# Weight sums of the first and the last chunk in a seven-product SwiGLU: other queue, other tiles, other order

## The chip, the core and the metric

The kernel runs on one core of a Trainium2 chip. The core has a matrix engine (TensorE, PE in the profile), a vector engine (VectorE, DVE), a scalar engine (ScalarE, ACT), GpSimd (POOL) and SyncE (SP), each with a queue of its own that it works through in order, and 16 DMA engines. [...] The metric is the device time of one execution in microseconds; the profile gives times within one execution, from the start of its span.

## The reference

The reference is an encoder trunk of two layers on one sequence of 512 tokens with 1024 features, in float32. Layer 0 mixes tokens with dilated window attention, layer 1 with a gated linear attention (GLA) in both directions. Behind each mixer stands a SwiGLU feed-forward network (FFN) with 2816 hidden features:

```python
for i in range(DEPTH):
    hn = rms_norm(h, attn_norm[i])
    h = h + mixer_i(hn)
    h = h + swiglu(rms_norm(h, ffn_norm[i]), ffn_w_gate_up[i], ffn_w_down[i])

def swiglu(h, w_gate_up, w_down):
    g, u = jnp.split(h @ w_gate_up, 2, axis=-1)
    return (jax.nn.silu(g) * u) @ w_down
```

## The kernel before

**Precision.** Each float32 operand is split into a high part (an ACT copy with rounding) and a low part (a DVE subtraction): `split`, L90 and L91. A product is three matmuls: high by high (L297), low weight by high (L298) and high weight by low (L299). Split weights live in three buffers each, `wh` and `wl`, so the split of a weight tile can run at most three tiles ahead of PE.

**Seven products.** `gate_up` computes `h @ [gate, up]` in six chunks of hidden features: chunks 0 to 4 of 512, chunk 5 (the last) of 256. A chunk is treated as a 2 by 2 block product, the tokens and the features of `h` being halved, and done with seven instead of eight block products of the Strassen kind. On the side of `h` the operands are A11, A12, A22 (pieces of `xs`) and four sums S1 to S4. On the side of the weights, DRAM holds four blocks for each chunk, and the sums of them are formed on the chip. In the order of the loop the products are:

| product | operand of h | weight, by `forms` | how the weight comes |
|---|---|---|---|
| 1 | A11 | `first` | chunk 0 and last: block 0 into `wf`; others: `wA` |
| 2 | A12 | `second` | block 1 into `wf` |
| 3 | S1 | `fifth` | `wA` = block 0 + block 2 |
| 4 | S2 | `sixth` | `wA` += `wC` (block 3), on DVE, L265 |
| 5 | S4 | `third` | `wC` (block 3); `wA` += block 1 is issued |
| 6 | S3 | `seventh` | `wB` = block 3 + block 2 |
| 7 | A22 | `fourth` | `wA` |

A product is 24 matmuls; weight tiles come in pairs of 128x1024. Loads are plain DMAs issued by SP (L225). Sums with a block from DRAM are DMAs that accumulate into the tile, issued by POOL (L230). An add waits until its tile's earlier load has landed and its earlier readers are done; all DMAs of POOL stand in one queue.

**The sums S1 to S4.** They are built once for each layer (`block_sums`), for four feature tiles of `h`: one ACT copy, four DVE operations of 256 columns and one split of 1024 columns for each tile, `sh` and `sl`. S1 to S4 of a tile are then ready together.

**Norm.** RMS norm is applied as a factor for each token behind the products. `add_square` sums squares of `h` into `acc` (ACT and DVE), `token_norm` sums over partitions on PE (L202) and takes the inverse root with small DVE and ACT steps (L108, L109 on ACT). The silu of each chunk (L356, L378), the product with the up half (L368, L380) and the four sums of partial results (L355, L367, L373) follow on ACT and DVE. `turn` transposes the finished half chunk on PE (L323) while the next chunk's products run.

**What sets the order.** The program is written once in the order above; a scheduler then orders each engine's queue by priority. `high_priority(offset=n)` moves what is issued inside it forward by n steps of the program; every `forms` step runs with AHEAD = 100, the first step of chunk 0 with 200 more. `issue_after(x)` keeps what is issued inside it behind instruction x. Tiles of a tag rotate through a fixed number of buffers, and a new phase (attention, FFN, GLA) lays its pools over those of the phase before; a tile that lies over an older one waits for that one's last reader. After the seven products `h` is stored to DRAM (`h_dram`, L352, by POOL), as its tiles are used for activations, and read back in `down`.

The lines that the prediction names: L90, L91 split; L97 load of other weights; L108, L109, L202, L205 norm; L150 sum of squares; L191 to L194 block sums; L225 load; L230 accumulating load; L265 sum of two weight tiles; L297 to L299 matmuls; L323 transposes; L337 copies of partial results; L352 store of `h`; L355, L356, L367, L368 sums, silu and product. L702 to L720 are attention, L784 is the residual sum behind the output projection.

Of the kernel before, what the change touches and what calls it, by code (L numbers as in the profile page):

```python
# [34 lines left out]
AHEAD = 100  # L35


class Trunk:
    def __init__(self, ctx, tc, ins):
        self.tc = tc  # L40
        self.nc = tc.nc
        self.ins = ins
        self.base = ctx.enter_context(tc.tile_pool(name="base", bufs=1))
# [9 lines left out]
    FFN = {"a": NH - KT, "sh": 4, "sl": 4, "wA": 4, "wB": 2, "g": 7, "Rc": 8}  # L53
# [4 lines left out]
    @contextmanager  # L58
    def phase(self, name, bufs):
        self.bufs = bufs  # L60
        with self.tc.tile_pool(name=name, bufs=1, reuse_waits="tile") as self.local:
            yield

    def t(self, tag, shape=(P, S), dt=F32):
        self.n += 1
        pool, bufs = (self.base, self.BASE) if tag in self.BASE else (self.local, self.bufs)
        return pool.tile(list(shape), dt, tag=tag, name=f"{tag}_{self.n}", bufs=bufs[tag])
# [18 lines left out]
    def split(self, src, shape, tag_h, tag_l):  # L86
        nc = self.nc
        hi = self.t(tag_h, shape, F32R)
        lo = self.t(tag_l, shape, F32R)
        nc.scalar.activation(hi, src, AF.Copy)  # L90
        nc.vector.tensor_sub(lo, src, hi.bitcast(F32))  # L91
        return hi, lo
# [89 lines left out]
    def block_sums(self, m):  # L182
        nc = self.nc
        stt = nc.vector.scalar_tensor_tensor
        c1 = self.cols[:, self.col0 + m:self.col0 + m + 1]
        c2 = self.cols[:, self.col0 + m + 4:self.col0 + m + 5]
        h2 = self.h[m + 4]
        t = self.t("g", (P, S))
        nc.scalar.activation(t, self.h[m], AF.Copy, scale=c1)
        f = self.t("g", (P, 4, 256))  # L190
        stt(f[:, 1], h2[:, 256:S], c2, t[:, 256:S], op0=ALU.mult, op1=ALU.subtract)  # L191
        nc.vector.tensor_sub(f[:, 0], t[:, 0:256], t[:, 256:S])
        stt(f[:, 2], f[:, 1], -1.0, t[:, 0:256], op0=ALU.mult, op1=ALU.subtract)
        stt(f[:, 3], h2[:, 0:256], self.minus[:, m:m + 1], f[:, 2], op0=ALU.mult, op1=ALU.subtract)  # L194
        hi, lo = self.split(f.rearrange("p a b -> p (a b)"), (P, 1024), "sh", "sl")
        return [(hi[:, i * 256:(i + 1) * 256], lo[:, i * 256:(i + 1) * 256]) for i in range(4)]

    def token_norm(self):
        nc = self.nc
        ss = self.p("t")  # L200
        for i in range(NT):
            nc.tensor.matmul(ss[:, i:i + 1], lhsT=self.acc[:, i * P:(i + 1) * P], rhs=self.ones[:, 0:1].bitcast(F32),  # L202
                             start=True, stop=True)
        v, r, tmp = (self.t("Rc", (P, 8)) for _ in range(3))
# [11 lines left out]
    def forms(self, dram, own, ahead=0):  # L216
        nc = self.nc
        n = dram.shape[1]
        raw = {}

        def load(block, tag, at=None):
            raw[tag] = []
            for i in range(n):
                w = self.t(at or tag, (P, 1024))
                nc.sync.dma_start(w, dram[block, i])  # L225
                raw[tag].append(w)

        def add(tag, block):
            for i in range(n):
                nc.gpsimd.dma_start(raw[tag][i], dram[block, i], accum_op=ALU.add)  # L230
# [19 lines left out]
        def second():  # L250
            if own:
                sums()
# [48 lines left out]
    def gate_up(self, layer, acts):  # L301
# [4 lines left out]
        weights.append(self.forms(self.ins["gate_up_last"][layer], True))  # L306
        first = next(weights[0])
        self.minus = self.t("Rc", (P, 8))
        DVE.tensor_scalar(self.minus[:, 0:4], self.cols[:, self.col0 + 4:self.col0 + 8], -1.0, None, op0=ALU.mult)
        sums = [self.block_sums(m) for m in range(KT // 2)]  # L310
# [3 lines left out]
        S3, S1, S2, S4 = ([s[i] for s in sums] for i in range(4))  # L314
# [13 lines left out]
        for j in range(6):  # L328
# [18 lines left out]
            if j == 0:  # L347
                for m in range(KT):
                    self.add_square(m, self.h[m], ("sq", "R")[m % 2])
                R = self.token_norm()  # L350
                for m in range(KT):
                    nc.gpsimd.dma_start(self.kept[m], self.h[m])  # L352
            for i in range(2):
                e = g1[:, i, 0:width]
                DVE.tensor_add(e, b2[i][:, 0:width], e)  # L355
                silu = ACT(e, e, AF.Silu, scale=R[:, i:i + 1])  # L356
            b3 = pair("s")
            self.product(b3, S1, next(w), width, True)
            turn(2)
            p5 = copy(b3)  # L360
            self.product(b1, S2, next(w), width, False)
            turn(3)
            h1 = copy(b1)
# [10 lines left out]
            self.product(b1, A22, next(w), width, False)  # L374
# [703 lines left out]
```

## Time and profile before

| | before |
|---|---|
| median of 3 runs (lowest to highest) | 1588.37 us (1587.5 to 1588.47) |
| profiled execution, own time | 1583.12 us |
| its span | 1581.0 us |
| mean granted clock of TensorE | 0.995 |
| DMA over the span | 183.93 MB, mean 116 GB/s |
| FFN of layer 0, first product / layer 1 | 626.6 us / 1224.7 us |

Rows of the timeline read: start, duration, engine, line, operation, written tile <- read tiles, shape, how many in a row, and in brackets the idle time before it with what ended that. Rows of the table of stretches give for each engine the busy time and (x) the instructions, then the granted clock, the share of time in which the DMA engines are busy, and GB/s. Durations of matmuls overlap: they follow each other every 0.227 us (512 wide). A row of DMAs by queue ends with the median time from issue to landing.

### The profile page before, as it was taken

To read this page: it belongs to the slowest core of one execution; us is meant where nothing else is said; L and a number is where in the kernel's file an instruction comes from. 1 tells how busy PE (TensorE), PEld (TensorE's weight loads), DVE (VectorE), ACT (ScalarE), POOL (GpSimd) and SP (SyncE) were. 2 spreads that over 40 slices of the span, in tenths; PEclk is the share of its full clock that TensorE was granted. 3 is DMA by queue.
4 is the path that set the end of the run, shared out by engine and by line. 5 is a ranking of instruction groups with operands and counts; after the bars stand their busy time and mean duration, and the time that the engine had idled before them with its cause. 6 is when DMAs were issued, how large, how long until landed. Compare 5 with 4: busy or idle time off the path is not lost.

```text
span 1581.0 us, 21074 instructions
## 1 busy us (share of the span) xinstructions
PE 1545.3 (98%) x8078; PEld 1256.1 (79%) x8078; DVE 948.3 (60%) x1714; ACT 778.0 (49%) x1319; POOL 104.1 (7%) x180
## 2 busy tenths in 40 slices
PE   8999999999999999799999999999999999999999
PEld 6878787887877878688878888777778788878887
DVE  6574656667467656766657533756666866648321
ACT  6343443445355554565547422554564765547211
POOL 0001010101000001011110000000001011110000
PEclk9999999999999999999999999999999999999999
DMA  7422222243221214867674332321128567674332
GB/s 272 146 70 81 80 81 80 68 131 89 80 68 48 71 44 156 230 136 172 159 161 116 100 99 85 108 67 57 64 77 268 150 157 169 155 155 118 99 120 65
DMA packets 60116, 183.93 MB, mean 116 GB/s; under 512 B 10064, under 2 KB 10640, under 8 KB 60016
## 3 DMA queue, kind: packets, MB, share of 16 engines
q1 hardware_dynamic: 46928, 139.46, 27.4%
q0 software_dynamic: 13088, 43.13, 14.3%
q8 instruction: 63, 1.03, 0.3%
q14 instruction: 37, 0.30, 0.1%
HBM read 174.11 MB, written 8.46 MB: 115 GB/s over the span
## 4 chain that ended last, share of the span: by engine, by line
PE 81%; DVE 8%; DMA 5%; ACT 3%; issue 2%; POOL 0%; SPq 0%; POOLq 0%; ACTq 0%; DVEq 0%
PE ppp L513 8%; PE ppp L511 8%; PE ppp L102 8%; PE ppp L103 8%; PE ppp L512 8%; PE ppp L104 8%; PE ppp L297 5%; PE ppp L299 4%; PE ppp L298 4%; PE po L620 4%; DMA wA<-in_gate_up_dram 2%; DVE wl L91 2%; PE ps L297 2%; PE ps L299 2%; PE ps L298 2%
## 5 line engine op out<-in xcount | busy, mean ns | idle before, releaser
L91 DVE TENSOR_TENSOR wl<-wf,wh 128x1024 fp32r<-128x1024 f32 (+1 forms) x186 | 220.8, 1187 | 216.0 <-ACT wh L90 215.1
L90 ACT ACTIVATE wh<-wf 128x1024 fp32r<-128x1024 f32 (+1 forms) x186 | 191.8, 1031 | 308.7 <-PE ppp L103 177.7
L511 PE MATMUL ppp<-wh,xs 128*128 128x512 f32 (+1 forms) x672 | 262.6, 393 | 5.7 <-ACT wh L90 5.7
L512 PE MATMUL ppp<-wl,xs 128*128 128x512 f32 (+1 forms) x672 | 262.3, 390 | 0.0
L513 PE MATMUL ppp<-wh,xs 128*128 128x512 f32 (+1 forms) x672 | 262.2, 390 | 0.0
L511 PEld LDWEIGHTS ppp<-wh,xs 128*128 128x128 f32 x672 | 127.6, 190 | 30.4 <-ACT wh L90 5.7
L513 PEld LDWEIGHTS ppp<-wh,xs 128*128 128x128 f32 x672 | 127.6, 190 | 23.2 <-issue 0.2
L512 PEld LDWEIGHTS ppp<-wl,xs 128*128 128x128 f32 x672 | 128.1, 191 | 22.0 <-DVE wl L91 1.2
L91 DVE TENSOR_TENSOR wl<-wA,wh 128x1024 fp32r<-128x1024 f32 x88 | 107.4, 1222 | 57.4 <-ACT wh L90 57.1
L90 ACT ACTIVATE wh<-wA 128x1024 fp32r<-128x1024 f32 x88 | 92.8, 1056 | 69.1 <-PE ppp L299 39.0
L297 PE MATMUL ppp<-wh,xs 128*128 128x512 f32 (+1 forms) x288 | 107.8, 380 | 3.6 <-ACT g L337 3.6
L299 PE MATMUL ppp<-wh,xs 128*128 128x512 f32 (+1 forms) x288 | 107.3, 372 | 0.0
L298 PE MATMUL ppp<-wl,xs 128*128 128x512 f32 (+1 forms) x288 | 107.1, 372 | 0.0
L103 PE MATMUL ppp<-xs,wh 128*128 128x512 f32 x256 | 103.6, 405 | 1.0 <-DVE xs L91 1.0
L102 PE MATMUL ppp<-xs,wh 128*128 128x512 f32 x256 | 103.4, 405 | 0.0
L104 PE MATMUL ppp<-xs,wl 128*128 128x512 f32 x256 | 102.7, 401 | 0.0
L91 DVE TENSOR_TENSOR wl<-wB,wh 128x1024 fp32r<-128x1024 f32 x38 | 46.5, 1225 | 72.7 <-ACT wh L90 72.7
L297 PE MATMUL ps<-wh,sh 128*128 128x512 f32 (+1 forms) x192 | 74.4, 388 | 7.1 <-ACT sh L90 4.9
L585 ACT ACTIVATE sm<-sm,st 128x160 f32<-128x160 f32 (+2 forms) x128 | 56.9, 446 | 43.0 <-DVE st L584 41.5
L298 PE MATMUL ps<-wl,sh 128*128 128x512 f32 (+1 forms) x192 | 73.3, 382 | 4.7 <-DVE wl L91 4.7
L298 PE MATMUL ppp<-wl,sh 128*128 128x512 f32 (+1 forms) x192 | 72.5, 378 | 1.8 <-DVE wl L91 1.8
L297 PE MATMUL ppp<-wh,sh 128*128 128x512 f32 (+1 forms) x192 | 73.0, 381 | 0.8 <-ACT wh L90 0.7
(310 smaller groups left out, 3087.3 us busy)
## 6 DMA issues: line engine op xcount, KB each, us to landing
wA<-in_gate_up_dram POOLq DMA_DIRECT2D x44, 512.0 KB, 5.5
wf<-in_down_dram SPq DMA_DIRECT2D x32, 512.0 KB, 3.6
wf<-in_gate_up_dram SPq DMA_DIRECT2D x24, 512.0 KB, 4.5
wA<-in_gate_up_dram SPq DMA_DIRECT2D x24, 512.0 KB, 4.3
wf<-in_a_w_v_dram SPq DMA_DIRECT2D x20, 512.0 KB, 3.8
wB<-in_gate_up_dram SPq DMA_DIRECT2D x20, 512.0 KB, 4.5
wf<-in_a_w_q_dram SPq DMA_DIRECT2D x16, 512.0 KB, 3.4
wf<-in_a_w_qk_dram SPq DMA_DIRECT2D x16, 512.0 KB, 3.4
```

What stands on the lines that cost most here:

```text
L90: nc.scalar.activation(hi, src, AF.Copy)
L91: nc.vector.tensor_sub(lo, src, hi.bitcast(F32))
L102: mm(out, lhsT=wh, rhs=xh, start=start, stop=False)
L103: mm(out, lhsT=wh, rhs=xl, start=False, stop=False)
L104: mm(out, lhsT=wl, rhs=xh, start=False, stop=stop)
L297: mm(a, lhsT=xh[:, tok], rhs=wh[:, f], start=start and k == 0, stop=False, skip_group_check=True)
L298: mm(a, lhsT=xh[:, tok], rhs=wl[:, f], start=False, stop=False, skip_group_check=True)
L299: mm(a, lhsT=xl[:, tok], rhs=wh[:, f], start=False, stop=k == last, skip_group_check=True)
L511: mm(a, lhsT=xh, rhs=wh[:, f], start=k == 0, stop=False)
L512: mm(a, lhsT=xh, rhs=wl[:, f], start=False, stop=False)
L513: mm(a, lhsT=xl, rhs=wh[:, f], start=False, stop=k == KT - 1)
L620: self.nc.tensor.matmul(o, lhsT=pts[b][c], rhs=vals(i0 + b, c), start=c == 0, stop=c == 1)
```

## The change

The diff has four parts, cut to their core:

```diff
-    FFN = {"a": NH - KT, "sh": 4, "sl": 4, "wA": 4, "wB": 2, "g": 7, "Rc": 8}
+    FFN = {"Rc": 4, "wB": 2, "a": NH - KT}
+    MIX = {"wA": 4, "sh": 4, "sl": 4, "g": 7}
...
-        with self.phase(f"ffn{layer}", self.FFN):
+        with self.phase(f"ffn{layer}", self.FFN), self.phase(f"mix{layer}", self.MIX):
...
-        def sums():
-            load(0, "wA")
+        def sums(queue=nc.sync):
+            load(0, "wA", queue=queue)
             add("wA", 2)
-            load(3, "wB")
-            raw["wC"] = raw["wB"]
-            load(3, "wB", "wA")
+            load(3, "wB", "wA", queue=queue)
             add("wB", 2)
+            summed = raw["wB"]
+            load(3, "wB", queue=queue)
+            raw["wC"], raw["wB"] = raw["wB"], summed
 
         def first():
+            if own and ahead:
+                with self.tc.high_priority(offset=OUT):
+                    sums(nc.gpsimd)
...
         def second():
-            if own:
-                sums()
+            if own and not started:
+                with self.tc.issue_after(self.added.ins):
+                    sums()
```

`own` is true for chunk 0 and the last chunk, `ahead` (and `started`) for chunk 0 alone, and OUT is 300. The six loads of chunk 0's sums are issued by POOL instead of SP. The FFN's pools are split in two and ordered anew, with `Rc` widened to 256 columns, so that these tiles lie over others of attention or GLA. The last chunk's sums are issued behind `self.added`, the latest add so far. The second part makes the block sums in three steps:

```diff
-        sums = [self.block_sums(m) for m in range(KT // 2)]
+        blocks = self.block_sums()
+        S1, S2, S3, S4 = next(blocks)
...
+        def parts(m, i, n=1):
+            e = f[m][:, i:i + n]
+            self.on_act = nc.scalar.activation(hi[m][:, i:i + n], e, AF.Copy)
+            self.on_dve = nc.vector.tensor_sub(lo[m][:, i:i + n], e, hi[m][:, i:i + n].bitcast(F32))
+
+        for m in half:
+            nc.scalar.activation(f[m][:, 2:4], self.h[m].rearrange("p (a b) -> p a b", b=256), AF.Copy, scale=c[m])
+            stt(f[m][:, 0], self.h[m + 4][:, 256:S], c[m + 4], f[m][:, 3], op0=ALU.mult, op1=ALU.subtract)
+            parts(m, 0)
+        yield [[(hi[m][:, i], lo[m][:, i]) for m in half] for i in range(4)]
+        for m in half:
+            stt(f[m][:, 1], f[m][:, 0], -1.0, f[m][:, 2], op0=ALU.mult, op1=ALU.subtract)
+            parts(m, 1)
+        yield
+        for m in half:
+            nc.vector.tensor_sub(f[m][:, 2], f[m][:, 2], f[m][:, 3])
+            stt(f[m][:, 3], self.h[m + 4][:, 0:256], self.minus[:, m:m + 1], f[m][:, 1],
+                op0=ALU.mult, op1=ALU.subtract)
+            parts(m, 2, 2)
```

In `gate_up`, S2 is made behind the splits for product 3, S3 and S4 behind those for product 4. The squares, the norm and the stores of `h` of chunk 0 move from between products 2 and 3 to the places below, and chunk 0's first silu behind the norm:

```diff
+            x5 = next(w)
+            if j == 0:
+                with self.tc.issue_after(self.low.ins):
+                    next(blocks)
+            self.product(b3, S1, x5, width, True)
...
+            x6 = next(w)
+            if j == 0:
+                next(blocks)
+                with self.tc.issue_after(self.on_act.ins), self.tc.issue_after(self.on_dve.ins):
+                    for m in range(KT):
+                        self.add_square(m, self.h[m], ("sq", "R")[m % 2])
+            self.product(b1, S2, x6, width, False)
             turn(3)
+            if j == 0:
+                R = self.token_norm()
...
+            x4 = next(w)
+            if j == 0:
+                with self.tc.issue_after(self.added.ins):
+                    for m in range(KT):
+                        nc.gpsimd.dma_start(self.kept[m], self.h[m])
+            self.product(b1, A22, x4, width, False)
```

POOL's queue at the entry of layer 0's FFN, before: the last memset of attention, the stores of `h`, and the first adds.

```order
L589 MEMSET sm_5536 128x64
L352 DMA h_dram_5971<-h_5581 128x512
L352 DMA h_dram_5971<-h_5583 128x512
L352 DMA h_dram_5971<-h_5585 128x512
L352 DMA h_dram_5971<-h_5587 128x512
L352 DMA h_dram_5971<-h_5589 128x512
L352 DMA h_dram_5971<-h_5591 128x512
L352 DMA h_dram_5971<-h_5593 128x512
L352 DMA h_dram_5971<-h_5595 128x512
L230 DMA wA_6003<-in_gate_up_dram 128x1024
L230 DMA wA_6005<-in_gate_up_dram 128x1024
```

And in the changed kernel, whose loads are L245 and whose adds L250 (wA_5917 and wA_5919 are `wA`, wA_5923 and wA_5925 the sum `wB`, wB_5929 and wB_5931 are `wC`):

```order
L629 MEMSET sm_5536 128x64
L245 DMA wA_5917<-in_gate_up_dram 128x1024
L245 DMA wA_5919<-in_gate_up_dram 128x1024
L245 DMA wA_5923<-in_gate_up_dram 128x1024
L250 DMA wA_5917<-in_gate_up_dram 128x1024
L250 DMA wA_5919<-in_gate_up_dram 128x1024
L245 DMA wA_5925<-in_gate_up_dram 128x1024
L250 DMA wA_5923<-in_gate_up_dram 128x1024
L245 DMA wB_5929<-in_gate_up_dram 128x1024
L250 DMA wA_5925<-in_gate_up_dram 128x1024
L245 DMA wB_5931<-in_gate_up_dram 128x1024
```

Six loads and four adds stand right behind the memset; the eight stores follow later, behind the second adds to wA_5917 and wA_5919. Layer 1 is alike.

POOL's queue around chunk 4 of layer 0, before (`in_gate_up_last_dram` is the last chunk's weight):

```order
L230 DMA wA_1423_7564<-in_gate_up_last_dram 128x1024
L230 DMA wA_1358_7209<-in_gate_up_dram 128x1024
L230 DMA wA_1425_7569<-in_gate_up_last_dram 128x1024
L230 DMA wA_1359_7211<-in_gate_up_dram 128x1024
L230 DMA wA_1358_7209<-in_gate_up_dram 128x1024
L230 DMA wA_1359_7211<-in_gate_up_dram 128x1024
L230 DMA wB_1379_7308<-in_gate_up_dram 128x1024
L230 DMA wB_1380_7310<-in_gate_up_dram 128x1024
L230 DMA wA_1423_7564<-in_gate_up_last_dram 128x1024
```

The same place in the changed kernel:

```order
L250 DMA wA_1354_7224<-in_gate_up_dram 128x1024
L250 DMA wA_1355_7226<-in_gate_up_dram 128x1024
L250 DMA wA_1354_7224<-in_gate_up_dram 128x1024
L250 DMA wA_1355_7226<-in_gate_up_dram 128x1024
L250 DMA wB_1375_7323<-in_gate_up_dram 128x1024
L250 DMA wB_1376_7325<-in_gate_up_dram 128x1024
L250 DMA wA_1419_7579<-in_gate_up_last_dram 128x1024
L250 DMA wA_1420_7582<-in_gate_up_last_dram 128x1024
L250 DMA wA_1419_7579<-in_gate_up_last_dram 128x1024
```

The last chunk's adds have moved from before and between chunk 4's adds to behind them.

DVE's queue in the changed kernel at the entry of layer 0's FFN, from the third low half of S2 to the second sum of weight tiles (L290 is the sum `wA` += `wC`, L207 to L212 are block sums, L199 low halves of them, L96 a low half of a weight):

```order
L199 TENSOR_TENSOR sl_1138_5952<-g_1142_5956,sh_1134_5948 128x256
L290 TENSOR_TENSOR wA_1120_5917<-wA_1120_5917,wB_1124_5929 128x1024
L207 SCALAR_TENSOR_TENSOR g_1143_5957<-g_1143_5957 128x256
L211 TENSOR_TENSOR g_1140_5954<-g_1140_5954 128x256
L211 TENSOR_TENSOR g_1141_5955<-g_1141_5955 128x256
L212 SCALAR_TENSOR_TENSOR g_1140_5954<-h_1057_5589,Rc_1119_5916,g_1140_5954 128x256
L96 TENSOR_TENSOR wl_1163_6096<-wA_1120_5917,wh_1162_6095 128x1024
L290 TENSOR_TENSOR wA_1121_5919<-wA_1121_5919,wB_1125_5931 128x1024
```

The sum that product 4 needs, and its low half (wl_1163), stand among the pieces of S2, S3 and S4 that were made at once, one tile after another, before.

More of the change, by code (lines that the diff above doesn't have):

```diff
@@ L90, in split @@
         nc.scalar.activation(hi, src, AF.Copy)
-        nc.vector.tensor_sub(lo, src, hi.bitcast(F32))
+        self.low = nc.vector.tensor_sub(lo, src, hi.bitcast(F32))
         return hi, lo
@@ L203, in token_norm @@
                              start=True, stop=True)
-        v, r, tmp = (self.t("Rc", (P, 8)) for _ in range(3))
+        v, r, tmp = (self.t("Rc", (P, 256)) for _ in range(3))
         nc.vector.tensor_scalar(v[:, 0:4], ss[:, 0:4], 1.0 / D, EPS, op0=ALU.mult, op1=ALU.add)
@@ L219, in forms, with load @@
         raw = {}
-        def load(block, tag, at=None):
+        started = ahead
+        def load(block, tag, at=None, queue=nc.sync):
             raw[tag] = []
@@ L224, in load @@
                 w = self.t(at or tag, (P, 1024))
-                nc.sync.dma_start(w, dram[block, i])
+                queue.dma_start(w, dram[block, i])
                 raw[tag].append(w)
```

54 lines of the change are left out of this document (23 added, 31 removed).

## The prediction

> **What bounds the kernel now.** I read the page first, then the table of stretches, the timeline at the edges of chunks, and last the rows around the gaps. The products of a chunk are numbered in the order of the loop: 1 (A11), 2 (A12), 3 (S1), 4 (S2), 5 (S4), 6 (S3), 7 (A22); layers are 0 and 1. First the page: busy time by engine, and the chain that ended last by engine.
>
> ```profile
> PE 1545.3 (98%) x8078; PEld 1256.1 (79%) x8078; DVE 948.3 (60%) x1714; ACT 778.0 (49%) x1319; POOL 104.1 (7%) x180
> ```
>
> PE is busy 98% of the span, so only its idle stretches and half-clock stretches can be won. The table of stretches shows where these lie in the FFNs (columns: PE, weight loads, DVE, ACT and POOL busy, granted clock, DMA share, GB/s).
>
> ```profile
> 600.00:626.00 26.00, 26.00 (x118) 21.43 (x118) 16.98 (x24) 10.77 (x16) 3.03 (x6) 1.00 0.47 154
> 626.00:650.00 24.00, 16.13 (x63) 12.61 (x62) 17.50 (x30) 11.90 (x16) 4.82 (x7) 0.86 1.04 312
> 714.00:754.00 40.00, 40.00 (x185) 32.82 (x184) 25.71 (x27) 23.28 (x31) 5.15 (x6) 1.00 0.72 171
> 794.00:842.00 48.00, 43.42 (x185) 33.89 (x185) 26.87 (x29) 24.23 (x33) 6.98 (x8) 0.96 0.65 142
> 1400.00:1442.00 42.00, 36.77 (x184) 29.83 (x183) 26.72 (x31) 24.60 (x34) 4.08 (x5) 0.96 0.47 107
> ```
>
> An ordinary chunk (714 to 754) leaves PE no idle time. The entry of layer 0's FFN leaves 7.9 us in 24 at a clock of 0.86; chunk 4 of each layer loses 4.6 and 5.2 us at 0.96. The exact losses come from the timeline of PE: the first matmul of products 1 and 7 of chunk 0 in layer 0 and in layer 1, then product 7 of chunks 2, 3 and 4 in layer 0 and in layer 1.
>
> ```profile
> 626.60 0.39 PE L297 MATMUL ppp<-wh,xs 128*128 128x512 f32 x1
> 673.50 0.48 PE L297 MATMUL ppp<-wh,xs 128*128 128x512 f32 x1
> 1224.66 0.39 PE L297 MATMUL ppp<-wh,xs 128*128 128x512 f32 x1
> 1259.71 0.50 PE L297 MATMUL ppp<-wh,xs 128*128 128x512 f32 x1
> 753.55 0.50 PE L297 MATMUL ppp<-wh,xs 128*128 128x512 f32 x1
> 793.79 0.50 PE L297 MATMUL ppp<-wh,xs 128*128 128x512 f32 x1
> 841.82 0.50 PE L297 MATMUL ppp<-wh,xs 128*128 128x512 f32 x1 [1.42 <-ACT g L337]
> 1340.17 0.50 PE L297 MATMUL ppp<-wh,xs 128*128 128x512 f32 x1
> 1380.40 0.50 PE L297 MATMUL ppp<-wh,xs 128*128 128x512 f32 x1
> 1428.71 0.50 PE L297 MATMUL ppp<-wh,xs 128*128 128x512 f32 x1 [2.17 <-ACT g L337]
> ```
>
> Products 1 to 6 of chunk 0 take 46.90 us in layer 0 and 35.05 in layer 1: **11.85 us** more. From product 7 to product 7 takes 40.24 us, and then 48.03, in layer 0 (**7.8 us** lost), and 40.23 and 48.31 in layer 1 (**8.1 us** lost). These 27.7 us are what the change can reach. The rows around the gaps name the causes: at the entry, SP's load of the first weight sum, POOL's accumulating add of the second half, ACT's split, the first matmul of product 3; then chunk 3's first add, chunk 4's first add, and ACT's split in chunk 4.
>
> ```profile
> 624.22 0.92 SPq L225 DMA_DIRECT2D wA<-in_gate_up_dram  x2
> 640.10 0.86 POOL L230 DMA_DIRECT2D wA<-in_gate_up_dram  x1 [7.69 <-DMA wA<-in_gate_up_dram]
> 640.26 1.06 ACT L90 ACTIVATE wh<-wA 128x1024 fp32r<-128x1024 f32 x1 [8.46 <-DMA wA<-in_gate_up_dram]
> 642.31 0.73 PE L297 MATMUL ps<-wh,sh 128*128 128x512 f32 x2 [4.67 <-ACT sh L90]
> 756.72 0.86 POOL L230 DMA_DIRECT2D wA<-in_gate_up_dram  x1 [13.69 <-DVE wl L91]
> 798.43 1.24 POOL L230 DMA_DIRECT2D wA<-in_gate_up_dram  x1
> 800.04 1.41 POOL L230 DMA_DIRECT2D wA<-in_gate_up_dram  x1
> 813.60 2.01 ACT L90 ACTIVATE wh<-wA 128x1024 fp32r<-128x1024 f32 x2 [5.44 <-DMA wA<-in_gate_up_dram]
> ```
>
> **The change part by part.** *Early sums at the entry of layer 0.* Six loads leave SP, and POOL issues them with their adds before its h_dram stores. The last attention transposes (from the chain of waits), the last matmul of product 2, POOL's row at that place, and the transfer times by issuing queue:
>
> ```profile
> 600.66 0.45 PE pt L720 x4
> 637.25 0.39 PE L299 MATMUL ppp<-wh,xs 128*128 128x512 f32 x1
> 618.91 0.56 POOL L352 DMA_DIRECT2D h_dram<-h  x1 [32.17 <-DVE h L784]
> wA<-in_gate_up_dram POOLq DMA_DIRECT2D x44, 512.0 KB, 5.5
> wA<-in_gate_up_dram SPq DMA_DIRECT2D x24, 512.0 KB, 4.3
> ```
>
> POOL stands idle for 32.17 us up to 618.91, so ten issues of 0.86 us (8.6 us) find room there. Today the loads start at 624.22, and the split waits until 640.26. In the new program the first four loads lie over tiles whose last readers are the softmax and these transposes; issued by 601.1, load and add (two times 5.5 us) end near 612. Product 3 then follows product 2 at 637.48, one step of 0.23 us behind its last matmul. The two loads of block 3 into wB wait for the last matmul of the output projection, just before 626.60; with 0.9 us of issue each and 5.5 us of flight they land by 634, and product 4's DVE sum wants them at 641.4. SP's 12 issues per kernel cost nothing either way: SP is not waited for at the entry except through these loads.
>
> *What is late next.* With the weights there, DVE sets products 4 to 6. Durations are spacings of queued instructions in the timeline of DVE:
>
> ```profile
> 642.29 2.36 DVE L91 TENSOR_TENSOR sl<-g,sh 128x1024 fp32r<-128x1024 f32 x2 [6.49 <-ACT sh L90]
> 644.57 0.48 DVE L194 SCALAR_TENSOR_TENSOR g<-h,Rc,g 128x256 f32<-128x256 f32 x1
> 644.97 2.35 DVE L91 TENSOR_TENSOR wl<-wA,wh 128x1024 fp32r<-128x1024 f32 x2
> 648.77 0.42 DVE L192 TENSOR_TENSOR g<-g 128x256 f32<-128x256 f32 x1
> 649.10 0.42 DVE L193 SCALAR_TENSOR_TENSOR g<-g,g 128x256 f32<-128x256 f32 x1
> 655.51 0.69 DVE L150 TENSOR_TENSOR acc<-acc,sq 128x512 f32<-128x512 f32 x1
> 656.11 0.68 DVE L355 TENSOR_TENSOR g<-ppp,g 128x512 f32<-128x512 f32 x1
> ```
>
> That is 1.14 us for 1024 wide, 0.60 for 512, 0.34 for 256, 0.40 for a 256-wide one with a column. From 637.0, when wl of product 3 is done, the new order puts on DVE, up to the low half that product 4's third matmul needs: two gate additions (1.20), one wl (1.14), three S2 parts and three low halves (2.04), the sum wA+=wC (1.14), three S4 and S3 pieces (1.02), one with a column (0.40), the wl itself (1.14): 8.1 us, to 645.1. Product 3 ends at 642.9 and two matmuls pass, so PE waits about **1.9 us**, and 0.45 more in products 4 and 5, where each next wl is as late. Bounds: nothing, if DVE gains time before 637; 5 us, if its work up to product 6 (19.5 us by the same spacings, against three products of 5.45) is all exposed. I take 1.9 + 0.45. Entry of layer 0: 11.85 - 2.35 = **9.5 us**.
>
> A stall can also lower the clock. The two adjoining 3.4 us stretches in chunk 4:
>
> ```profile
> 830.67:834.09 3.42, 1.92 (x8) 1.04 (x7) 1.23 (x1) 2.03 (x3) 0.00 (x0) 1.00 0.66 125
> 834.09:837.50 3.41, 3.41 (x10) 2.67 (x9) 2.04 (x3) 1.84 (x3) 0.00 (x0) 0.50 0.47 150
> ```
>
> PE was busy 1.92 of 3.42 us in one stretch and got half the clock in the next, which costs 1.7 us. A stall of 1.9 us can do the same if it falls inside one stretch; I leave this to the upper side. [...]
>
> *Adds of the last chunk queued last.* Chunk 4's first add is at 756.72 + 40.24 = 796.96 by the cadence, and comes at 798.43, side by side with an add of the last chunk; its second lands at 813.50, 13.5 us after issue, where 5.5 is usual, and ACT's split waits 5.44 us. Without these neighbours chunk 4 is an ordinary chunk. The last chunk's own adds follow those of chunk 4, near 824 by the cadence, and land near 830; its product 3 comes after product 7 (834.0) of chunk 4 and products 1 and 2 of half width, 834.0 + 5.5 + 2 x 2.8 = 845. Bounds: nothing won, if they only wait elsewhere, and the full 7.8 and 8.1 us; I take **7.6 and 7.9**, 0.2 below full each.
>
> *Norm and squares later, both layers.* In layer 0 the norm's matmuls (row L202 before) move into product 7; the squares then share ACT and DVE with product 6, and I put nothing on it beyond the above. In layer 1 there was no weight wait to win, and the norm's chain becomes late. ACT there:
>
> ```profile
> 1247.21 1.28 ACT L108 ACT_TABLE_LOAD   x1
> 1254.41 1.34 ACT L356 ACTIVATE g<-g,Rc 128x512 f32<-128x512 f32 x2
> ```
>
> Three such loads (for L108, L109 and the silu), 3.9 us together, two small activations of 0.2, half the silu row (0.7), the first product g (0.7) and six small steps on DVE (0.2 each and a little) make a chain of about 7.4 us from the norm on. PE has 27 matmuls of 0.227 us, 6.1 us, up to the transposes that need g: 1.3 us of wait. DVE's backlog of squares makes the norm itself wait about 1.3 us. Against that 0.6 us of small waits go from products 3 and 4 of layer 1. Net **-2.0 us**, bounds +1 (all hidden) and -4 (each wait doubled).
>
> *h_dram stores* move from before the sums to after chunk 0's last add. They hold POOL for eight times 0.56 us, and POOL is busy 5.15 us of 40 in a chunk, so they are hidden; behind a late add they would delay chunk 1's first adds by at most these 4.5 us.
>
> Sum: 9.5 + 7.6 + 7.9 - 2.0 = 23.0 us. The profiled execution took 1583.12 us, 1560.1 after; the median of the runs, 1588.37, lies 5.25 us above it, so **1565.4**.
>
> **The rivals.** *DVE and the clock take more.* The stall is 3.5 us, one half-clock stretch follows (1.7), and layer 1 pays 4: 9.5 - 1.6 - 1.7 + 15.5 - 4.0 = 17.7, time 1570.7. For it: DVE is at 17.5 of 24 us already in the entry, and at 60% overall; against: products 4, 5 and 6 are interleaved in the new order of PE.
>
> *The early sums are not early.* If POOL's first load waits for a tile freed only by the last attention matmul, loads start at 626 as today, and the entry wins nothing: 15.5 - 2.0 = 13.5, time 1574.9. A slow POOL queue has the same effect, if each of ten issues came 2 us late. For it: POOL keeps order, and one held load holds all behind it; POOL's transfers take 5.5 us against SP's 4.3. Against: 14 us of slack between 612 and 626. [...]
>
> *The last chunk's wait only moves* (its adds now block chunk 5 instead): 9.5 - 2.0 = 7.5, time 1580.9. Against: 15 us of slack.
>
> *Slower: the early sums take the DMA engines from the output projection's weights.* Ten transfers of 512 KB are 5.2 MB, 16.8 us at the 312 GB/s of the stretch 626 to 650. If they delayed each layer's projection weights by all that, PE would idle 33.6 us, and 33.6 - 23.0 leaves the kernel 10.6 us slower: 1599. It turns negative from 11.5 us of delay in each layer. Against: the stretch 600 to 626 uses 0.47 of the DMA engines at 154 GB/s, PE never waits there, and the queues share.
>
> *It doesn't do what it says* (the scheduler puts the waits back): about 1588.
>
> **How the numbers follow.** Forecast 0.61, DVE and clock 0.14, sums not early 0.08, last chunk moved 0.06, slower 0.07, no effect 0.04. The forecast's own range goes by its bounds (DVE exposed 5 us, layer 1 at -4: 1570; no new stall: 1560). It is widened by the next two cases to 1575, and by 2 us at both ends for the difference between profiled and timed runs: 1558 to 1577. Within 0.2% (3.2 us, about what a measurement can tell from no change) lies only the last case: faster 0.89, same 0.04, slower 0.07.
>
> **What would show it right or wrong.** Right: PE's product 3 near 637.5 with no gap, a gap near 643 to 646 released by DVE's wl, DVE without idle time from 637 to 657; product 7 to product 7 in 40.3 us for chunk 4; a wait for product g near the first transposes of layer 1. Wrong, if POOL's first wA load is later than 612, if a PE gap in the projection names wf, or if the last chunk's splits wait for wA.

## The result, and the profile after

| | before | after |
|---|---|---|
| median of the runs (lowest to highest) | 1588.36 us (1587.50 to 1588.47, 4 runs) | 1569.36 us (1568.11 to 1571.47, 4 runs) |
| profiled execution, own time | 1583.12 us | 1569.00 us |
| its span | 1581.0 us | 1567.2 us |
| mean granted clock | 0.995 | 0.996 |

The ratio is 0.9883, with a 95% interval of 0.9866 to 0.9900: the kernel is 19.0 us faster, where 23.0 were forecast. The two profiled executions differ by only 14.1 us; the other 4.9 us come from attention, as the last section shows.

The table of stretches of the changed kernel, for the entry of layer 0's FFN, an ordinary chunk, and chunk 4 of layers 0 and 1 (the columns are those of before):

```profile
631.00:655.00 24.00, 22.02 (x94) 17.00 (x93) 23.39 (x40) 18.36 (x30) 3.51 (x6) 1.00 0.51 148
655.00:679.00 24.00, 23.99 (x110) 19.59 (x108) 21.85 (x36) 18.81 (x28) 6.29 (x11) 1.00 0.95 284
709.64:749.88 40.24, 40.24 (x187) 32.99 (x185) 26.29 (x28) 23.51 (x30) 5.15 (x6) 1.00 0.71 170
790.36:832.07 41.71, 40.35 (x186) 33.03 (x185) 27.78 (x31) 24.59 (x33) 6.94 (x8) 1.00 0.74 164
1373.00:1414.67 41.67, 40.31 (x185) 32.99 (x184) 27.05 (x30) 24.59 (x33) 6.93 (x8) 1.00 0.75 164
```

PE's idle time at the entry falls from 7.9 us to 2.0 in 24, and DVE is busy 23.39 of those 24: the engine that bounds this stretch has changed. Chunk 4 keeps 1.36 us of idle time in each layer, and there is no half clock in any of these rows. PE's timeline gives the lengths: the first matmul of product 1, then of product 7 in chunks 0 and 1, for layer 0 and layer 1; then of product 7 in chunks 3 and 4 for layer 0 and layer 1.

```profile
631.38 0.39 PE L322 MATMUL ppp<-wh,xs 128*128 128x512 f32 x1
667.25 0.50 PE L322 MATMUL ppp<-wh,xs 128*128 128x512 f32 x1
709.64 0.50 PE L322 MATMUL ppp<-wh,xs 128*128 128x512 f32 x1
1214.85 0.39 PE L322 MATMUL ppp<-wh,xs 128*128 128x512 f32 x1
1249.25 0.50 PE L322 MATMUL ppp<-wh,xs 128*128 128x512 f32 x1 [1.22 <-ACT wh L95]
1292.55 0.50 PE L322 MATMUL ppp<-wh,xs 128*128 128x512 f32 x1
790.36 0.51 PE L322 MATMUL ppp<-wh,xs 128*128 128x512 f32 x1
832.07 0.50 PE L322 MATMUL ppp<-wh,xs 128*128 128x512 f32 x1 [1.36 <-ACT g L362]
1373.00 0.50 PE L322 MATMUL ppp<-wh,xs 128*128 128x512 f32 x1
1414.67 0.50 PE L322 MATMUL ppp<-wh,xs 128*128 128x512 f32 x1 [1.36 <-ACT g L362]
```

Read in the same way for every kernel below, in us:

| | start of FFN 0 | layer 0: products 1-6 | layer 0: 7 to 7, chunk 0 to 1 | layer 0: chunk 4 | layer 1: products 1-6 | layer 1: 7 to 7, chunk 0 to 1 | layer 1: chunk 4 |
|---|---|---|---|---|---|---|---|
| before | 626.6 | 46.90 | 39.84 | 48.03 | 35.05 | 40.25 | 48.31 |
| after | 631.4 | 35.88 | 42.39 | 41.71 | 34.40 | 43.30 | 41.67 |
| difference | +4.8 | -11.02 | +2.55 | -6.32 | -0.65 | +3.05 | -6.64 |

The six FFN columns sum to -19.0 us, the difference of the medians. All other stretches behind attention agree within 0.3 us. (In the variants below, a stage of unchanged program repeats within about 0.5 us as long as the clock is full.) The 42.39 and 43.30 us contain the norm's matmuls (about 0.9 us), which before stood within products 1 to 6. The table goes on for the variants at the end of the experiments.

At the entry of layer 0, the chain of waits of the changed kernel shows the new bound (start, duration, what):

```profile
642.35 0.68 DVE g L374
643.03 1.13 DVE wl L96
644.17 0.60 DVE g L374
644.77 1.00 DVE g L207 x3
645.77 1.00 DVE sl L199 x3
646.77 1.14 DVE wA L290
647.91 0.34 DVE g L207
648.25 0.67 DVE g L211 x2
648.92 0.40 DVE g L212
649.31 1.15 DVE wl L96
650.46 0.04 issue
650.50 0.50 PE ppp L323
```

From 642.35 to 650.46 there is nothing but DVE: 8.1 us, instruction for instruction the list of the prediction. The early sums themselves are in POOL's timeline:

```profile
599.81 1.09 POOL L245 DMA_DIRECT2D wA<-in_gate_up_dram  x2 [8.27 <-DVE mw L741]
606.72 1.82 POOL L250 DMA_DIRECT2D wA<-in_gate_up_dram  x2
612.12 0.85 POOL L250 DMA_DIRECT2D wA<-in_gate_up_dram  x1 [3.03 <-DMA wA<-in_gate_up_dram]
631.62 0.56 POOL L245 DMA_DIRECT2D wB<-in_gate_up_dram  x1 [18.65 <-PE ppp L109]
```

The sums start at 599.81 and `wC` at 631.62, behind the output projection; product 3 follows product 2 without a gap.

### The profile page after: what moved, and what is told of

The parts are those of the page before. It is cut to its first block, busy times and chain, and to the rows that moved or that the text cites. A ratio compares the mean times of both kernels' runs of the same rounds, so it can differ in the third digit from the quotient of the medians.

```text
span 1567.2 us, 21097 instructions
## 1 busy us (share of the span) xinstructions
PE 1543.7 (98%) x8078; PEld 1256.3 (80%) x8078; DVE 949.6 (61%) x1730; ACT 780.3 (50%) x1335; POOL 110.8 (7%) x192
## 4 chain that ended last, share of the span: by engine, by line
PE 85%; DVE 7%; ACT 4%; DMA 2%; issue 2%; SPq 0%; ACTq 0%; DVEq 0%
PE ppp L553 8%; PE ppp L551 8%; PE ppp L552 8%; PE ppp L107 8%; PE ppp L108 8%; PE ppp L109 8%; PE ppp L322 6%; PE ppp L323 6%; PE ppp L324 5%; PE po L660 4%; PE ps L322 2%; PE ps L324 2%; PE ps L323 2%; DVE wl L96 2%; ACT wh L95 2%; PE ps L728 2%
## 5 line engine op out<-in xcount | busy, mean ns | idle before, releaser
L96 DVE TENSOR_TENSOR wl<-wf,wh 128x1024 fp32r<-128x1024 f32 (+1 forms) x186 | 220.9, 1188 | 214.3 <-ACT wh L95 213.1
L96 DVE TENSOR_TENSOR wl<-wA,wh 128x1024 fp32r<-128x1024 f32 x88 | 107.5, 1222 | 38.3 <-ACT wh L95 38.0
L96 DVE TENSOR_TENSOR wl<-wB,wh 128x1024 fp32r<-128x1024 f32 x38 | 46.5, 1225 | 70.6 <-ACT wh L95 70.6
L624 DVE CUSTOM_DVE_ANT_0 sm<-ps,masks 128x160 f32<-128x160 f32 (+2 forms) x128 | 39.6, 354 | 53.1 <-PE ps L728 31.6
```

Of the source, the lines that this page charges most:

```text
L96: self.low = nc.vector.tensor_sub(lo, src, hi.bitcast(F32))
```

## The experiments

Each run's "before" is the kernel before on the same chip; its medians were 1590.2, 1591.1 and 1591.4 us in the three sessions, with single runs from 1585.5 to 1595.7. Where a few us count, the stages of the profiles decide.

**One part alone: the last chunk.** Only the placing of the last chunk's sums is put into the kernel before.

```diff
-            if own:
+            if own and started:
+                sums()
+            elif own:
+                with self.tc.issue_after(self.added.ins):
                     sums()
```

> The kernel before with one part of the change alone: the last chunk's sums are issued behind the latest add. Theory (the parts add up, and the last chunk's adds delayed those of chunk 4): from product 7 of chunk 3 to product 7 of chunk 4 takes 41.7 us in both layers, as in the changed kernel, where 48.0 and 48.3 stood before; 13.0 us faster, about 1575.4. The entry of layer 0 keeps its 46.9 us. Rival (the wait only moves): chunk 4 is mended and the last chunk, product 7 to product 7, rises from 25.0 us to 30 or more; 0 to 3 us faster. A second reading rides on this run: its program up to the FFN of layer 0 is that of before, so if its attention part takes 631 us instead of 626.6, the 4.8 us that attention seems to lose in the changed kernel are no effect of the change.

Measured: 1575.76 us, ratio 0.9902 (0.9871 to 0.9932). Chunk 4 takes 41.62 and 42.32 us, the entry 47.22. Chunk 5 stays at 24.98 in layer 0 and rises to 26.54 in layer 1. So the last chunk's adds did delay chunk 4; against the kernel before, the medians differ by 14.4 us and the stages behind attention by 10.5 (this profile has one half-clock stretch more at the entry than that of before, and one in chunk 5 of layer 1). The rest of the wait did not go: product 7 of chunk 4 in layer 0 reads

```profile
838.56 0.50 PE L301 MATMUL ppp<-wh,xs 128*128 128x512 f32 x1 [1.29 <-ACT g L341]
```

with 1.29 us for a copy on ACT, no DMA; in layer 1 the same wait is 1.92 us, which makes the 42.32. And this program, the same as before up to the FFN, starts that FFN at 629.4, not 626.6.

**The other part alone: the entry.** In the changed kernel the last chunk's sums are placed as before.

```diff
-                with self.tc.issue_after(self.added.ins):
-                    sums()
+                sums()
```

> The changed kernel without the part on the last chunk: its sums are queued by priority alone, as before. Theory (the parts add up): the entry of layer 0 stays at about 35.9 us for products 1 to 6 and 42.4 from product 7 to product 7, chunk 4 is back at 48 us in both layers; about 6 us faster than before, 1582.3. Rival (the early sums at the entry also relieve chunk 4, by the other queue and tiles): chunk 4 stays near 42 us and the time near 1570.

Measured: 1586.44 us, ratio 0.9976 (0.9961 to 0.9991). Products 1 to 6 of layer 0 take 36.93 us, chunk 4 is back at 48.72 and 49.35. Faster by 3.7 us instead of 6. Chunk 4 goes the theory's way. Where the rest of the gain went is seen in the stages: 44.90 us instead of 43.3 in layer 1 and 26.58 instead of 24.95 in its chunk 5, each with a half-clock stretch that the changed kernel's profile lacks; by the stages of this one profile nothing is left of the gain. By medians the parts add up, 14.4 + 3.7 = 18.1 against 19.0.

**The early loads from SP.**

```diff
-                    sums(nc.gpsimd)
+                    sums()
```

> The changed kernel with chunk 0's six loads issued by SP instead of GpSimd, at the same priority and into the same tiles. Theory (the queue counts: on SP they stand behind the loads of wf, which wait for splits of the output projection): the first wA load is issued near 620 instead of 599.8, product 3 of layer 0 waits again, products 1 to 6 take 42 to 47 us; 6 to 11 us slower than the changed kernel, 1575 to 1580. Rival (only the freed tiles and the priority count): within 1 us of the changed kernel, 1569.

Measured: 1575.03 us, ratio 0.9901 (0.9872 to 0.9930), at the lower end of the range expected; its interval overlaps that of the changed kernel, so the stages decide. Products 1 to 6 of layer 0 take 43.09 us, 7.2 more than with POOL. Of these, 3.9 us are longer waits of PE (5.9 us in all, at products 3, 4 and 7, against 2.0); most of the rest is a half clock from 639.79 to 646.62, right behind the wait at product 3. SP's queue and PE at product 3:

```profile
609.90 14.22 SPq L245 DMA_DIRECT2D wf<-in_gate_up_dram  x4
624.28 2.06 SPq L245 DMA_DIRECT2D wA<-in_gate_up_dram  x4
639.65 0.69 PE L322 MATMUL ps<-wh,sh 128*128 128x512 f32 x1 [1.99 <-ACT wh L95]
```

The loads of `wA` stand behind four of `wf`, which wait for buffers until 624, and so they start where they started before. The queue matters, not the freed tiles alone. The start came out at 624.28, not near 620, and the stage is still 3.8 us shorter than before. Layer 1, where tiles and queue are free early in either way, takes 34.41 and 43.35 us, the same as with POOL.

**The sum wA+=wC on GpSimd.**

```diff
-                nc.vector.tensor_add(raw["wA"][i], raw["wA"][i], raw["wC"][i])
+                (nc.gpsimd if started else nc.vector).tensor_add(raw["wA"][i], raw["wA"][i], raw["wC"][i])
```

> The changed kernel with the two sums wA+=wC of chunk 0 done by GpSimd instead of VectorE, in both layers. Theory (DVE's queue sets products 4 to 6 at the entry of layer 0): if GpSimd needs no more than about 2.5 us for one, the gaps of 1.11 and 0.66 us at product 4 shrink to under 0.6 together, products 1 to 6 take 34.7 instead of 35.9 us, and the kernel is 1 to 1.5 us faster than the changed one, about 1568. If GpSimd needs 4 us or more, product 4 waits for it and the kernel is 1 to 4 us slower. Rival (ACT's queue holds the split, not DVE): the gap at product 4 stays within 0.2 us although the sum is off DVE and done in time.

Measured: 1573.31 us, ratio 0.9891 (0.9864 to 0.9918); products 1 to 6 of layer 0 take 42.98 us, 7.1 more, of which the next step gives 1.8 back (40.63 us). All expectations missed this size. Some of it is the clock: this profile has two half-clock stretches from 651.73 to 658.55, behind the long gap shown below. The sum took 2.40 us on GpSimd and was done in time; what suffered was DVE (first POOL's, then DVE's timeline, then PE's at product 4):

```profile
641.37 2.40 POOL L290 TENSOR_TENSOR wA<-wA,wB 128x1024 f32<-128x1024 f32 x1 [8.91 <-DVE wl L96]
644.94 2.40 POOL L290 TENSOR_TENSOR wA<-wA,wB 128x1024 f32<-128x1024 f32 x1 [1.17 <-DVE wl L96]
...
641.80 3.06 DVE L96 TENSOR_TENSOR wl<-wA,wh 128x1024 fp32r<-128x1024 f32 x1
645.38 2.92 DVE L207 SCALAR_TENSOR_TENSOR g<-g 128x256 f32<-128x256 f32 x3
...
652.76 1.22 PE L322 MATMUL ppp<-wh,sh 128*128 128x512 f32 x2 [5.01 <-ACT wh L95]
```

DVE's subtraction beside the first sum takes 3.06 us instead of 1.22, and three block sums beside the second 2.92 instead of 1.09: 3.7 us of DVE lost, against 2.3 taken off it. The scheduler also put the splits for product 4 behind block sums on ACT, and the gap grew to 5.0 us. That DVE's time is what counts here fits; the run does not isolate it, since the order and the clock changed as well.

**Less on DVE before product 4.** The two gate additions of chunk 0 (1.2 us) are moved.

```diff
+            for i in range(2 if j > 0 else 0):
...
                 next(blocks)
+                with self.tc.issue_after(self.on_dve.ins):
+                    for i in range(2):
+                        DVE.tensor_add(g1[:, i], b2[i], g1[:, i])
```

> The changed kernel with chunk 0's two gate additions (0.60 us each on DVE, before the block sum S2) moved behind the splits for product 6. Nothing else leaves or joins DVE. Theory (DVE's queue sets product 4 at the entry of layer 0): the gaps of 1.11 and 0.66 us at product 4 lose 1.2 us together, to under 0.7, and products 1 to 6 take 34.7 instead of 35.9 us; 1 us faster than the changed kernel. Rival (ACT's own queue, with its copies and splits, holds product 4): the gap stays within 0.3 us of 1.77.

Measured: 1570.78 us, ratio 0.9885 (0.9856 to 0.9915), no change against the changed kernel. The gaps went from 1.77 to 1.48 us, the rival's size. Its ACT timeline, with the copy of product 3 and then the split for product 4:

```profile
644.91 0.60 ACT L362 ACTIVATE g<-ps 128x512 f32<-128x512 f32 x1 [1.03 <-PE ps L324]
645.41 1.05 ACT L95 ACTIVATE wh<-wA 128x1024 fp32r<-128x1024 f32 x1
```

DVE has finished the sum at 644.90, but the copy waits for product 3 and stands ahead of the split. A second bound lies right behind the first. What is won there is also lost again later: the transposes now wait 1.34 us (layer 0) and 1.60 us (layer 1) for the product g, and the step from product 7 to 7 grows by 1.1 and 1.8 us (with one half-clock stretch in layer 1).

**Both at once.** In addition the copy of product 3 is placed behind that split.

```diff
+            if j == 0:
+                x6 = next(w)
+                with self.tc.issue_after(self.highs[0].ins):
+                    p5 = copy(b3)
+                next(blocks)
```

> The kernel with chunk 0's gate additions later, and besides ACT's two copies of product 3 behind the first split for product 4 (in chunk 0 only). Theory (two bounds lie one behind the other at product 4: DVE's queue, and then ACT's copy of product 3 ahead of the split): the sum of weights is ready near 1 us before product 3 ends, so the split starts there and the gap before product 4 goes from 0.95 to under 0.4 us; products 1 to 6 of layer 0 take about 35.2 instead of 36.2 us. Rival (the split cannot start earlier because its buffer is freed late, by product 3's matmuls): the gap stays near 0.95 us.

Measured: 1568.13 us (one run). The gap before product 4 falls from 0.95 to 0.61 us, and with the low half's 0.63 the two gaps make 1.24 us instead of 1.77; products 1 to 6 take 35.82 us, as little as the changed kernel's 35.88 within what they vary. So both bounds are real, each worth some tenths, and lifting both gave 0.5 us at the gap and nothing that lasts in the stage. The rival is out: ACT's split waits for DVE's sum, not for its buffer. That sum was ready at 647.11, only 0.2 us ahead of the last matmul of product 3, not 1 us as expected.

**The rest of chunk 4.**

```diff
+            if j == 4:
+                copied = self.copied
...
-        with self.tc.high_priority(offset=AHEAD):
+        with self.tc.high_priority(offset=AHEAD), self.tc.issue_after(copied.ins):
             early += [
```

> The changed kernel with ACT's early splits for the down projection (wA and wB from h) placed behind the last copy of product 6 in chunk 4. Theory (the 1.4 us that chunk 4 still loses is ACT's order: an early split waits for DVE and stands ahead of a weight split and of the copy that product 7 needs): product 7 of chunk 3 to product 7 of chunk 4 takes 40.3 instead of 41.7 us in both layers; 2.7 us faster. Rival (the last chunk's adds still hold chunk 4 a little): it stays at 41.7. A third way: the early splits become late for the down projection, and the last part (product 7 of chunk 5 to the end) grows by 1 us or more.

Measured: 1567.72 us, ratio 0.9860 (0.9835 to 0.9885); chunk 4 takes 40.21 and 40.20 us, and product 7 has no gap. This is ACT in the changed kernel around that place:

```profile
829.95 0.63 ACT L438 ACTIVATE wA<-h 128x512 fp32r<-128x512 f32 x1 [1.41 <-DVE wl L96]
830.49 1.04 ACT L95 ACTIVATE wh<-wA 128x1024 fp32r<-128x1024 f32 x1
831.44 0.58 ACT L362 ACTIVATE g<-ppp 128x512 f32<-128x512 f32 x1
```

An early split for the down projection (L438) waits 1.41 us for DVE and holds the weight split and the copy behind it; the copy comes 0.9 us after product 6 has ended. Chunk 5 grew by 0.5 us in layer 0 and 0.1 in layer 1, so 2.4 of the 3.0 us stay.

**The norm of layer 1 as before.**

```diff
+            if j == 0 and layer == 1:
+                for m in range(KT):
+                    self.add_square(m, self.h[m], ("sq", "R")[m % 2])
+                R = self.token_norm()
```

> The changed kernel with the squares, the norm and the first silu of layer 1 back between products 2 and 3, and layer 0 as changed. Theory (in layer 1 the later norm costs 2.4 us): product 7 of chunk 0 to product 7 of chunk 1 goes from 43.3 back to 40.3 us, products 1 to 6 take 35 us; 2.4 us faster than the changed kernel. Rival (the later block sums, not the norm, cost it): products 1 to 6 of layer 1 rise above 37 us, as squares and block sums now meet on DVE before product 4, and the gain is under 1 us.

Measured: 1567.08 us, ratio 0.9858 (0.9830 to 0.9885). The step from product 7 to 7 is 40.25 us again (3.05 won), and products 1 to 6 rise from 34.40 to 36.44 (2.04 lost, 0.9 of it the norm's matmuls): 1.0 us net; the median lies 2.3 us below the first of the changed kernel, and attention took 3.5 us less in this profile. Theory and rival are each right in one of the columns. The late norm had waited behind ACT's squares and the table loads (three of 1.28 us each in the changed kernel); put early, it makes the high and low halves of S2 to S4 late (four gaps, 1.5 us together).

**All three, and the best two.** The first combination joins gate additions, early splits and norm; the second leaves the gate additions.

> All three together: gate additions of layer 0 later, early splits behind the copy, norm of layer 1 back. Theory (three separate waits, so the gains add): 1.1 + 2.7 + 2.4 = 6.2 us faster than the changed kernel, about 1563. Rival (they share ACT and DVE and hide one another): 3 us or less.

Measured: 1566.37 us, ratio 0.9850 (0.9806 to 0.9894): 3.0 us below the changed kernel's first median, the rival's figure. Measured against its own runs of before the gain looks larger (ratio 0.9850 against 0.9883), but the stages behind attention also give 3.0 us (932.9 against 935.9). They say why: early splits and norm give what they give alone, and the gate additions cost 0.9 us from product 7 to 7 in layer 0 (43.33).

> The changed kernel with the early splits of the down projection behind the copy in chunk 4, and layer 1's norm back between products 2 and 3. Theory (waits in different places, so the gains of the two add): 3.0 + 1.0 = 4.0 us faster than the changed kernel run beside it, with 40.2 us for chunk 4 in both layers and 36.4 + 40.3 us for the entry of layer 1. Rival (they share ACT): 2 us or less.

> The changed kernel as it is, beside the one above. Theory (the stages of the FFNs repeat from run to run, and only attention varies by some us): 35.9 us for products 1 to 6 of layer 0, 41.7 us for chunk 4 in both layers, 34.4 + 43.3 for the entry of layer 1, each within 0.3 us; ratio to the kernel before 0.988 within 0.002. Rival (the first profile of before was typical and attention did become 4.8 us slower by the change): the attention part takes 631 us again, and that of the other variants with the same program up to there does, too.

Measured beside each other: 1566.64 us, ratio 0.9845 (0.9823 to 0.9866), for the two edits, and 1570.52 us, ratio 0.9872 (0.9857 to 0.9887), for the changed kernel again: 3.9 us apart, as expected, though the intervals touch. The changed kernel's stages come out alike, and its attention takes 632.6 us; why that does not decide for the rival is told in the last section. The best kernel of the study is the one with two edits more.

The table of stages for the variants:

| | start of FFN 0 | layer 0: products 1-6 | 7 to 7 | chunk 4 | layer 1: products 1-6 | 7 to 7 | chunk 4 |
|---|---|---|---|---|---|---|---|
| after, again | 632.6 | 35.91 | 42.44 | 41.63 | 34.44 | 43.39 | 41.59 |
| last chunk alone | 629.4 | 47.22 | 39.91 | 41.62 | 35.07 | 40.19 | 42.32 |
| entry alone | 629.5 | 36.93 | 42.44 | 48.72 | 34.44 | 44.90 | 49.35 |
| loads from SP | 626.6 | 43.09 | 42.16 | 41.65 | 34.41 | 43.35 | 41.86 |
| sum on GpSimd | 630.2 | 42.98 | 40.63 | 41.72 | 35.37 | 43.29 | 41.64 |
| gate later | 628.4 | 36.25 | 43.48 | 41.74 | 33.03 | 45.08 | 41.78 |
| gate and copy later | 630.8 | 35.82 | 43.40 | 41.72 | 33.04 | 43.57 | 41.56 |
| early splits later | 631.2 | 37.01 | 42.42 | 40.21 | 34.43 | 43.31 | 40.20 |
| norm 1 back | 627.9 | 36.37 | 42.43 | 41.79 | 36.44 | 40.25 | 41.77 |
| all three | 633.2 | 35.70 | 43.33 | 40.21 | 36.44 | 40.27 | 40.20 |
| best two | 631.9 | 37.02 | 42.44 | 40.20 | 36.44 | 40.21 | 40.23 |

## Why the prediction was right

The direction and the mechanism hold, and the time lies in the range; 19 of the 23 us came. By its own steps:

- **Entry of layer 0** (9.5 us forecast, 8.5 measured: 11.02 less 2.55). The sums arrive, product 3 has no gap, and the stall of product 4 is DVE's 8.1 us as listed, 1.77 us in two gaps where 1.9 was forecast (its own figures, 645.1 less 642.9 and two matmuls, give 1.7). Behind it came 0.2 us at product 5 instead of 0.45. The larger gap is released by ACT's split, not by DVE's wl as the signs had it. One more bound stood behind it that the prediction did not name: ACT's copy of product 3 ahead of the split. The missing 1.0 us is in the step from product 7 of chunk 0 to that of chunk 1, where "I put nothing on it" was too little: beside the norm's matmuls, chunk 1 has a gap of 0.71 us at product 3, released by ACT's split. That the late norm and silu on ACT cause it is not shown, since no run puts the norm of layer 0 back; in layer 1 putting it back took 3.05 us away.
- **Last chunk** (7.6 and 7.9 us forecast, 6.3 and 6.6 measured). This is the term that was mis-sized: "0.2 below full each". Of the full loss 1.4 us in each layer was never the adds'. It was ACT's order, it stood in the row that the prediction quotes (1.42 and 2.17 us released by ACT's g, not by a DMA), and moving the early splits of the down projection took it away.
- **Layer 1** (-2.0 us forecast, -2.4 measured). The size is right, in part by luck. Of the chain the three table loads (1.28 us each) and the wait at the transposes are there, 0.8 us in three gaps where 1.3 was forecast. The other 1.3 us, DVE's backlog that delays the norm, came as a different wait of like size: 1.22 us at product 7, for a split that stands behind ACT's squares.
- **Stores of h.** Between the adds of chunk 0 and of chunk 1 they cost nothing that a row shows: chunk 1's first add (670.22) waits for DVE, and the last store was issued 9.5 us earlier.
- **The clock.** The half-clock stretch of the rival "DVE and the clock take more" did not come in the two profiles of the changed kernel, but it did in others, as the last section shows.

The rivals "the early sums are not early" and "the last chunk's wait only moves" are refuted for this kernel; the first is what happens with the loads on SP. POOL's queue was not slow either: its issues at the entry took 0.5 to 1.3 us each. The slower rival does not occur: PE has no gap over 0.15 us in the output projection.

## What to carry to other kernels

When a wait for data is removed, list what the next engine must do in that stretch, instruction by instruction with durations of the trace: here that list gave DVE's stretch of 8.1 us and, to 0.2 us, the stall behind it, and 23.39 busy us of DVE in 24 confirm it. Before a whole gap is booked on one cause, read the releaser of each piece of it: here a fifth was an ACT copy held up by an early split ahead of it. A load that must go early needs an issuing queue with nothing blocking ahead of it; with a higher priority on SP, whose queue waits for other buffers, the loads went out at 624.28 us as before, and with POOL at 599.81.

## What the runs showed of the hardware

**A sum on GpSimd holds up DVE.** Beside a 2.40 us sum on GpSimd, a DVE subtraction of 1024 columns took 3.06 us instead of 1.22 (rows above). Not every DVE instruction is held: layer 1 of the same run shows both kinds (POOL's second sum there, then DVE's timeline):

```profile
1230.60 2.39 POOL L290 TENSOR_TENSOR wA<-wA,wB 128x1024 f32<-128x1024 f32 x1 [1.17 <-DVE wl L96]
...
1230.44 1.27 DVE L374 TENSOR_TENSOR g<-ppp,g 128x512 f32<-128x512 f32 x2
1231.64 1.64 DVE L207 SCALAR_TENSOR_TENSOR g<-g 128x256 f32<-128x256 f32 x1
```

Two gate additions with one input in PSUM run beside the sum in their usual 0.6 us each; the block sum with both inputs in SBUF takes 1.64 us instead of 0.42 and ends 0.3 us after POOL's sum. The other held instructions fit a wait for the end of POOL's sum: the subtraction of 3.06 us ends 1.09 us behind it and the three block sums 0.96 us, about what they take alone (1.22 and 1.09 us). What holds the one kind and lets the other run is not shown. That GpSimd is slowed in turn is not shown: its four sums take 2.39 to 2.40 us each.

**The same stall sometimes halves the clock.** The gaps of about 1.12 and 0.66 us at product 4 are the same in six profiles; three have a half-clock stretch behind them, three have none. Where it comes, products 1 to 6 take 36.9 to 37.0 us instead of 35.9 to 36.4. The half-clock stretches begin whole multiples of 3.413 us apart, in the changed kernel (117.61, 199.53 and 295.10 us: 24 and 28 of them) as in before (117.29, 642.94, 834.09 and 1404.12 us: 154, 56 and 167), so each trace is cut here at points counted in this way from its own half-clock stretches. Two such stretches, one behind the other, of the kernel with the early splits later, and the same two of the changed kernel (columns of the table of stretches):

```profile
647.49:650.90 3.41, 1.63 (x6) 0.78 (x5) 3.41 (x7) 2.66 (x5) 0.33 (x1) 1.00 0.01 2
650.90:654.31 3.41, 3.41 (x10) 2.67 (x9) 3.41 (x6) 2.00 (x2) 0.66 (x2) 0.50 0.67 95
```

```profile
646.67:650.09 3.42, 2.06 (x8) 1.05 (x6) 3.42 (x7) 2.68 (x5) 0.00 (x0) 1.00 0.01 2
650.09:653.50 3.41, 3.00 (x12) 2.10 (x12) 3.41 (x6) 2.11 (x3) 0.86 (x1) 1.00 0.39 54
```

In the first kernel both gaps fall into one stretch, and PE is busy for 1.63 us of it; in the second a cut goes through the later gap. The other two profiles with a half clock have 1.67 and 1.79 busy us in that stretch, the other two without have at least 2.06 and 2.30 in each. So for this stall the half clock went with where the cuts fell: it came behind a stretch with 1.63 to 1.79 busy us, and not behind stretches with 2.06 and more. It is no sharp rule for others: 1.51 busy us in before (from 636.13) and 1.88 with the loads from SP (from 1414.62) were followed by full clock.

**Attention varies by some us from one execution to the next.** The start of layer 0's FFN lies between 626.6 and 633.2 us in the profiles, and the two programs that are the same up to there differ, too (626.6 before, 629.4 with the last chunk alone). The same 300 us of before, of after and of after again:

```profile
100.00:400.00 300.00, 299.88 (x1965) 240.17 (x1964) 190.58 (x494) 135.42 (x300) 27.34 (x55) 0.99 0.29 86
```

```profile
100.00:400.00 300.00, 300.00 (x1944) 240.28 (x1944) 188.87 (x492) 135.10 (x300) 27.43 (x55) 0.98 0.28 84
```

```profile
100.00:400.00 300.00, 299.99 (x1937) 239.82 (x1937) 187.77 (x491) 133.80 (x299) 27.32 (x55) 0.97 0.27 84
```

The fewer matmuls got through, the lower was the clock: attention draws a few half-clock stretches, more in one execution than in another. Up to the start of layer 0's FFN the traces have one of 3.41 us in before and with the loads from SP (626.6 us both), two where that start is 627.9 and 628.4, three at 629.4 and 629.5, and four to six from 630.2 to 633.2. So the start follows their number, in changed and unchanged programs alike. The profile of before has but one, and lies 5.2 us below the median of its own runs. The 4.8 us are also complete before anything that the change moves: a short wait of PE near the end of attention lies at 579.44 us before and at 584.23 after, and the first early load goes out at 599.81. They are therefore put down to the clock and not to the change, and a difference of two profiled executions is to be read stage by stage. What brings these stretches about in attention is open.
